# An encoder layer on one core: the order of everything outside the dense loop, chosen with another simulation

## The chip, the cores and the metric

One core of a Trainium2 chip runs the whole kernel. Its engines are TensorE (PE: matrix products), VectorE (DVE), ScalarE (ACT), GpSimd (POOL, here only for indirect loads) and SyncE (SP, here only for issuing DMAs). Each engine works through its own instruction queue in the order in which it was compiled, and waits at the head of that queue for the semaphores that the instruction needs. The metric is device time in microseconds (us) for one execution, as the median over runs.

## The reference

One layer of a streaming-encoder trunk for 1024 tokens of width 1024, in float32:

```
xn = rms_norm(h, norm1_g);  p = xn @ w_in          # split in xa, gate (512 each), us (512)
ya = rg_lru_group(xa, gate, ...)                   # conv, gates, first-order scan over time
yb = s5_group(us, ...)                             # state-space scan in chunks, GLU
h  = h + concat[rms_norm(ya), rms_norm(yb)] @ w_out
h  = h + peer_ffn(rms_norm(h))                     # below
out = rms_norm(h, normf_g)

# peer_ffn: 16384 single-neuron experts, 8 heads, 16 experts per token and head
q = x @ wq;  s1, s2 = q1 @ k1.T, q2 @ k2.T         # two sets of 128 scores per head
e, g = the 16 best of the sums s1 + s2, with softmax weights
act = gelu(u_tab[e] . x)
out = sum over (head, k) of g * act * v_tab[e]
```

## The kernel before, in words

The 1024 tokens are eight blocks of 128. Each block holds tokens of one half of the time axis, so that the second part can begin on the first half while the second half is still in work.

**Front** (`front`). The first norm, the input product, the S5 scan (`quarter`, four times), the LRU (`lru`, four times), the gates, the GLU, the two output norms and `w_out`. All large products are made in three passes from a high and a low part of each operand (`split_to`: ACT copies the high part, DVE subtracts to get the low one). `w_out` runs for the first four blocks, then the second half runs from `late`, `loads_late` and `norms_late`.

**PEER** (`peer`) works two ways. `NG` = 3 blocks are *gathered*: after the query and a top-k on DVE (`topk_gather`), POOL fetches one row of `peer_u` or `peer_v` per token and chosen expert by indirect DMA (tile `row`, eight buffers), and DVE multiplies and sums it (a `row` instruction for u; an accumulation into `hb` for v): 768 rows of 128 x 1024. `ND` = 5 blocks are *dense*: for these every expert is computed. `norm2` and `query` make `xDh`/`xDl` and the scores (`x2t`, `qp`, `S_d`), `build_g` makes the matrix of weights from one-hot tiles (`ohA`, `ohB`, `gp`, `gs`) and stores it in the DRAM tensor `G_d`, and `ahead` computes the activations of 97 of the 128 expert tiles beforehand (`ur` is loaded, split to `uh` and `ul`, multiplied into `ap`, evicted by ACT to `aa`, stored in the DRAM tensor `A_d`). The **dense loop** (`dense`) then runs over 32 groups of four tiles: it reads `A_d` back (`hr`), multiplies with the weights (`gt` from `G_d`, turned by ACT to `gq`), and multiplies by the rows of `peer_v` (`vp`, `total`). The rest of the gathered rows is spread through this loop.

What sets the order of the work:

- In the program text, the generators of the front and of PEER are merged by a planner (`Merge`), which has a cost for each kind of instruction, a clock for each engine and a bias for each generator; it always continues the one whose next step could start earliest. That gives the *trace order*.
- The tile framework then compiles the trace: outside blocks marked as manual, each engine's instructions are put in order by a list scheduler. It simulates the program, and whenever an engine is free it takes, of the instructions that the simulation holds ready, the one that stands first in the trace; one that is not ready is passed by. The same holds for the instructions that issue DMAs on the queues of SP, ACT and POOL. Buffers of the tile pools are handed out in that order too.
- The dense loop is written out by hand, and its order among its own instructions is kept:

```python
    mg.run([], until="g")
    weights(0)
    mg.run([], until="ahead")
    ...
    with tc.manual_schedule():
        dense()
```

All compute instructions pass one helper, so the profile gives them all line 146 and they are told apart by their tiles. Line 1170 is the indirect load, 1226 the load of `ur`, 1264 the store to `A_d`, 1131 the store to `G_d`, 1365 the reload `hr`, 1324 the load of `gt`, 1369 that of `vr`, 729 the load of the residual `h` on ACT's queue, 773 and 819 the loads of the weights of `w_out` and of the GLU, and 964 that of the query weights.

## Time and profile before

| | |
|---|---|
| Time, median of 3 runs | 2860.66 us (2846.72 to 2867.12) |
| The profiled execution | 2868.52 us, span 2866.7 us |
| Granted TensorE clock, mean | 0.944 |
| Busy: PE, DVE, ACT, POOL | 89%, 83%, 47%, 39% of the span |
| DMA | 767 MB, mean 268 GB/s |

The profile is of one execution. A row of a timeline has the start and the duration in us, then engine, line, operation, the written tile, the tiles read and how many were merged into the row; in square brackets stands the time for which the engine was idle before it and what ended that wait. A row of the waits has the waiting engine and tile, the one waited for, the total in us, how many times, and the longest. "q" behind an engine's name is its sequencer, which issues DMAs.

### The profile page before, as it was taken

The numbers are of one execution on the slowest core, as the hardware profiler recorded it, in microseconds if no ns is written. First come the engines' busy times: TensorE is split into PE (matmuls) and PEld (weight loads), VectorE is DVE, ScalarE is ACT, GpSimd is POOL, SyncE is SP. The second block draws the span as 40 slices with busy tenths as digits, with TensorE's granted clock in tenths as the row PEclk, the third lists the DMA queues.
The fourth block names the chain that finished last, engine by engine and source line by source line (L and its number), as shares of the span: only waits on it lengthen the run. The fifth ranks groups of instructions, "written<-read, shape, count | busy, mean of one in ns | idle before, by whom it ended". The sixth has DMA issues, their size and how long they took to land.

```text
span 2866.7 us, 40962 instructions
## 1 busy us (share of the span) xinstructions
PE 2549.5 (89%) x14623; PEld 2303.9 (80%) x14623; DVE 2383.2 (83%) x4582; ACT 1339.9 (47%) x2439; POOL 1131.2 (39%) x777
## 2 busy tenths in 40 slices
PE   6887787648889999899999968999899999999996
PEld 5765587448878899899989967888788888888884
DVE  7786543998889999999989847888788888988885
ACT  5355542122228568395774934443344443343332
POOL 0000000126825376673746533444344444444440
PEclk9989898869999999999999989999999999999998
DMA  5111444457969899899999988888789898988883
GB/s 163 25 28 33 124 144 130 153 181 238 383 240 338 286 362 386 320 371 362 361 363 316 346 314 274 312 314 315 274 311 316 314 313 312 328 316 310 312 310 106
DMA packets 305116, 767.21 MB, mean 268 GB/s; under 512 B 29328, under 2 KB 126928, under 8 KB 299792
## 3 DMA queue, kind: packets, MB, share of 16 engines
q0 software_dynamic: 110592, 402.70, 39.2%
q1 hardware_dynamic: 187168, 350.04, 35.2%
q10 hardware_dynamic: 7152, 11.85, 1.5%
q8 instruction: 115, 1.88, 0.2%
q14 instruction: 89, 0.73, 0.1%
HBM read 673.86 MB, written 89.46 MB: 266 GB/s over the span
## 4 chain that ended last, share of the span: by engine, by line
PE 58%; DVE 19%; DMA 11%; issue 6%; ACT 3%; POOL 2%; SPq 0%; ACTq 0%; DVEq 0%; POOLq 0%
PE vp L146 23%; PE ap L146 16%; PE total L146 6%; PE qp L146 3%; DMA A_d<-aa 3%; DVE row L146 3%; PE gp L146 3%; DVE ix L146 2%; POOL row L1170 2%; PE wop L146 1%; DMA ur<-in_uT_dram 1%; PE pj L146 1%; DVE ul L146 1%; DVE v L146 1%; DMA nf<-in_gf_dram 1%
## 5 line engine op out<-in xcount | busy, mean ns | idle before, releaser
L1170 POOL DMA_INDIRECT row<-in_peer_u_dram,idx x384 | 559.7, 1458 | 1037.6 <-DVE ix L146 505.8
L1170 POOL DMA_INDIRECT row<-in_peer_v_dram,idx x384 | 568.8, 1481 | 589.1 <-DVE hb L146 427.7
L146 PE MATMUL ap<-xDl,uh 128*128 128x320 f32 x2048 | 651.0, 318 | 54.7 <-ACT aa L146 32.8
L146 PE MATMUL ap<-xDh,ul 128*128 128x320 f32 x2048 | 643.3, 314 | 5.3 <-DVE ul L146 5.3
L146 PE MATMUL ap<-xDh,uh 128*128 128x320 f32 x2048 | 641.3, 313 | 0.3 <-issue 0.3
L146 DVE SCALAR_TENSOR_TENSOR hb<-row,act,hb 128x1024 f32<-128x1024 f32 x384 | 494.4, 1288 | 11.4 <-DMA row<-in_peer_v_dram,idx 4.6
L146 DVE CUSTOM_DVE_ANT_0 row<-row,xg 128x1024 f32<-128x1024 f32 x384 | 462.4, 1228 | 31.1 <-DMA row<-in_peer_u_dram,idx 20.5
L146 PEld LDWEIGHTS ap<-xDl,uh 128*128 128x128 f32 x2048 | 391.1, 191 | 58.7 <-ACT aa L146 35.3
L146 PE MATMUL vp<-vl,hh 128*128 128x512 f32 x1024 | 400.9, 391 | 15.2 <-DVE h L146 13.8
L146 PE MATMUL vp<-vh,hl 128*128 128x512 f32 x1024 | 400.5, 391 | 0.0
L146 PE MATMUL vp<-vh,hh 128*128 128x512 f32 x1024 | 400.2, 391 | 0.0
L146 PEld LDWEIGHTS ap<-xDh,ul 128*128 128x128 f32 x2048 | 390.6, 191 | 8.7 <-DVE ul L146 6.8
L146 PEld LDWEIGHTS ap<-xDh,uh 128*128 128x128 f32 x2048 | 389.8, 190 | 0.0
L146 ACT ACTIVATE gq<-gt 128x640 f32<-128x640 f32 x128 | 174.7, 1364 | 343.6 <-DVE hr L146 287.8
L146 DVE TENSOR_TENSOR ul<-ur,uh 128x1024 fp32r<-128x1024 f32 x128 | 157.3, 1229 | 104.7 <-ACT uh L146 104.6
L146 PEld LDWEIGHTS vp<-vl,hh 128*128 128x128 f32 x1024 | 193.3, 189 | 55.8 <-DVE h L146 14.7
L146 PEld LDWEIGHTS vp<-vh,hh 128*128 128x128 f32 x1024 | 193.4, 189 | 40.5
L146 PEld LDWEIGHTS vp<-vh,hl 128*128 128x128 f32 x1024 | 193.4, 189 | 39.4
L146 PE MATMUL gp<-ohB,ohA 128*128 128x128 f32 x1280 | 185.8, 281 | 29.5 <-DVE ohB L146 21.2
L146 ACT ACTIVATE ohB<-ohB,kt 128x128 f32<-128x128 f32 x480 | 206.8, 504 | 0.0
L146 ACT ACTIVATE aa<-ap 128x320 f32<-128x320 f32 x194 | 84.8, 440 | 246.7 <-PE ap L146 212.2
L146 PEld LDWEIGHTS gp<-ohB,ohA 128*128 128x128 f32 x1280 | 171.9, 195 | 34.0 <-issue 15.6
(415 smaller groups left out, 4626.9 us busy)
## 6 DMA issues: line engine op xcount, KB each, us to landing
ur<-in_uT_dram SPq DMA_DIRECT2D x128, 512.0 KB
vr<-in_peer_v_dram SPq DMA_DIRECT2D x128, 512.0 KB
G_d<-gs SPq DMA_DIRECT2D x20, 2048.0 KB
gt<-G_d SPq DMA_DIRECT2D x32, 1280.0 KB
A_d<-aa SPq DMA_DIRECT2D x97, 320.0 KB
hr<-A_d SPq DMA_DIRECT2D x96, 320.0 KB
wqr<-in_wq_dram SPq DMA_DIRECT2D x32, 512.0 KB
wor<-in_w_out_dram SPq DMA_DIRECT2D x32, 256.0 KB
```

Of the source, the lines that this page charges most:

```text
L146: return fn(*args, **kw)
L1170: G.indirect_dma_start(out=r, out_offset=None, in_=a["peer_v" if at >= P else "peer_u"], in_offset=bass.IndirectOffsetOnAxis(ap=idx[n][:, ...
```

## The change

The context that compiles the kernel is given one flag. With it the list scheduler drives another simulation: one that keeps a time line for each hardware resource (engines, queues, DMA engines) rather than the plain simulation of the cores. The program text, its trace order, all tiles and all buffer counts are the same; the dense loop is under manual schedule in both.

```diff
-    with _tile.TileContext(nc) as tc:
+    with _tile.TileContext(nc, schedule_with_timeline_sim=True) as tc:
         body(tc, args)
```

## The prediction

> **What bounds the kernel now.** I read the stretches of the span first, because the change leaves one part of the program alone and I need to know how long that part is. The columns are the stretch, then busy time and count on PE, its weight loads, DVE, ACT and POOL, the granted clock, the DMA share and GB/s.
>
> ```profile
> 0.00:290.00 290.00, 223.97 (x1360) 178.75 (x1360) 216.34 (x417) 141.43 (x229) 2.78 (x9) 0.91 0.23 64
> 290.00:475.00 185.00, 158.83 (x824) 143.83 (x824) 83.87 (x132) 85.48 (x145) 0.00 (x0) 0.92 0.43 128
> 475.00:610.00 135.00, 64.51 (x219) 48.29 (x220) 122.31 (x518) 26.90 (x40) 23.44 (x21) 0.71 0.49 167
> 610.00:790.00 180.00, 154.24 (x974) 148.19 (x973) 156.44 (x407) 42.16 (x90) 115.22 (x75) 0.91 0.79 281
> 790.00:1640.00 850.00, 795.78 (x5573) 787.23 (x5573) 803.39 (x2004) 565.32 (x1370) 488.78 (x312) 0.97 0.94 337
> 1640.00:1740.00 100.00, 63.98 (x403) 62.71 (x402) 52.92 (x54) 40.47 (x80) 33.61 (x25) 0.80 0.87 320
> 1740.00:2867.00 1127.00, 1088.21 (x5278) 934.89 (x5276) 947.89 (x1053) 438.14 (x487) 467.38 (x336) 0.98 0.84 296
> ```
>
> From about 1740 us the hand-written dense loop runs with PE busy 1088 of 1127 us; the order there is fixed, so it is worth nothing to this change. What the change can reach is 1740 us. In it PE is busy 224.0 + 158.8 + 64.5 + 154.2 + 795.8 + 64.0 = 1461 us, so 279 us are idle. The largest reachable stretch, 790 to 1640, has PE at 94%, DVE at 95% and the DMA engines at 94%: three resources full together, so another order has little to win there and something to lose. The loose places are 475 to 610 (PE 65 of 135) and the seam to the dense loop, 1640 to 1740 (PE 64 of 100).
>
> Next I looked for what an order can cause: an engine's queue whose head waits for a transfer while ready work stands behind it. At the seam, in the timelines of ACT, PE, SP and DVE:
>
> ```profile
> 1684.39 0.44 ACT L146 ACTIVATE aa<-ap 128x320 f32<-128x320 f32 x1 [2.13 <-PE ap L146]
> 1699.62 1.33 ACT L146 ACTIVATE gq<-gt 128x640 f32<-128x640 f32 x1 [14.80 <-DMA gt<-G_d]
> 1700.86 0.75 ACT L146 ACTIVATE aa<-ap 128x320 f32<-128x320 f32 x2
> 1701.33 0.64 PE L146 MATMUL ap<-xDl,uh 128*128 128x320 f32 x1 [9.94 <-ACT aa L146]
> 1701.31 7.17 SPq L1264 DMA_DIRECT2D A_d<-aa  x2
> 1710.45 0.80 SPq L1365 DMA_DIRECT2D hr<-A_d  x2
> 1713.72 0.83 DVE L146 TENSOR_TENSOR hr<-hr,gq 128x640 f32<-128x640 f32 x1 [30.21 <-DMA hr<-A_d]
> ```
>
> ACT stands 14.80 us before `gq<-gt`, the first copy of the dense loop, whose load has not landed. Two `aa` evictions of the pre-computed tiles stand behind it; PE waits 9.94 us for them. The last `A_d` stores therefore go out from 1701, the reload `hr<-A_d` at 1710, and DVE starts the dense loop after 30.21 us of waiting.
>
> The second place is the start of the dense blocks' norm:
>
> ```profile
> 573.67 0.75 DVE L146 SCALAR_TENSOR_TENSOR h<-wop,rg,h 128x512 f32<-128x512 f32 x1
> 575.62 1.06 ACT L146 ACTIVATE uh<-ur 128x1024 fp32r<-128x1024 f32 x1 [4.04 <-DMA ur<-in_uT_dram]
> 576.58 1.04 ACT L146 ACTIVATE jk<-h 128x1024 f32<-128x1024 f32 x1
> 581.25 0.17 DVE L146 TENSOR_SCALAR vv<-vv 128x5 f32<-128x5 f32 x1
> 583.79 1.06 ACT L146 ACTIVATE wqh<-wqr 128x1024 fp32r<-128x1024 f32 x1 [3.67 <-DMA wqr<-in_wq_dram]
> 584.88 1.23 DVE L146 TENSOR_TENSOR wql<-wqr,wqh 128x1024 fp32r<-128x1024 f32 x1 [3.34 <-ACT wqh L146]
> 586.03 0.16 DVE L146 TENSOR_TENSOR r<-r,vv 128x5 f32<-128x5 f32 x1
> 587.72 1.94 PE L146 MATMUL x2t<-ident,xn 128*128 128x128 f32 x8 [20.87 <-ACT wqh L146]
> 615.03 1.03 PE L146 MATMUL x2t<-ident,xn 128*128 128x128 f32 x8
> ```
>
> The last half of `h` is written at 574.4, but its square sum `jk` starts at 576.58, because a weight split `uh` that waited for its load is ahead of it: 2.2 us. The last factor of `r` is ready to compute at 581.4 and runs at 586.03, behind `wql`, which waits for a weight load: 4.6 us. PE has nothing for 20.87 us.
>
> **The change, part by part.** No arithmetic, tile, buffer count or DMA is added or removed. The dense block is written in manual order and keeps it. What moves is, on each engine and on the queues of SP, ACT and POOL, the place of instructions outside that block: the scheduler picks by trace order among what its simulation holds ready, and the change swaps the simulation that says when that is. The trace does not show the new order, so I bound its cost.
>
> Seam: if the finer simulation holds `gt` back for as long as the trace does, both `aa` go ahead of `gq`, and PE's last matmul group starts 9.94 us earlier; the `A_d` stores, the `hr` reload and the first dense product follow in a chain. `gq` is then late next: it still cannot start before 1699.6, and ends at 1700.9, which is earlier than `hr` would be (1713.7 − 9.9 = 1703.8), so the 9.9 us hold. Against a second seam delay stand the SP stores, shown by these rows of SP's timeline and one of the list of DMA issues:
>
> ```profile
> 1638.63 0.37 SPq L1131 DMA_DIRECT2D G_d<-gs  x1
> 1640.61 18.55 SPq L1264 DMA_DIRECT2D A_d<-aa  x1
> 1672.46 0.37 SPq L1131 DMA_DIRECT2D G_d<-gs  x1
> 1672.93 17.33 SPq L1264 DMA_DIRECT2D A_d<-aa  x1
> ...
> G_d<-gs SPq DMA_DIRECT2D x20, 2048.0 KB
> ```
>
> Each 2 MB `G_d` store makes the `A_d` issue behind it hold SP for 17 to 19 us, and the loads `ur`, `vr` and `gt` queue behind that. A new order can move these holds but not remove them; I cost them at nothing, covered as now by DVE's rows. [...]
>
> Norm: 2.2 + 4.6 = 6.8 us, if `jk` and `r` go ahead of the weight splits. DVE is 122 of 135 us busy here, but `r`, `xn` and `xDl` are short and come before everything PE can do next, so I take the 6.8 whole. If DVE puts rows or top-k steps in the freed place, nothing is left of it.
>
> Middle, 790 to 1640: here are PE's and ACT's waits of that stretch.
>
> ```profile
> PE gp L146 <- DVE ohB L146: 21.2, 4, 7.6
> PE ap L146 <- ACT aa L146: 19.0, 6, 7.9
> ACT aa L146 <- DMA A_d<-aa: 23.2, 4, 11.7
> ACT uh L146 <- DMA ur<-in_uT_dram: 10.2, 4, 8.0
> ```
>
> PE waits 19.0 us for `aa`, held in ACT's queue by a full store buffer. One of four such holds moved behind ready one-hot work would give about 5 us; I take 5. The ends are −19 (all of them) and +54, if the balance is lost and PE's idle time here (850 − 796 = 54) doubles; the value sits near zero because the engines are full.
>
> First 475 us: a hold of another kind stands there.
>
> ```profile
> 283.93 17.18 ACTq L729 DMA_DIRECT2D h<-in_x_dram  x16
> 301.15 0.63 ACT L146 ACTIVATE wgh<-wg 128x512 fp32r<-128x512 f32 x1 [16.17 <-DMA h<-in_x_dram]
> 303.88 0.77 PE L146 MATMUL wop<-wol,nh 128*128 128x512 f32 x1 [20.73 <-issue]
> ```
>
> Sixteen issues of `h` fill ACT's queue for 17.18 us while PE stands 20.73 us. They are earlier in trace order than `wgh` and ready together, so either simulation should pick them first: I cost this at 0. If the other simulation splits them up, it is worth up to 16 us.
>
> Sum: −9.9 − 6.8 − 5 = −21.7 us. The profiled execution took 2868.5 us for a span of 2866.7, and the sum makes it 2846.8. The median of the runs shown, 2860.66, lies 7.9 us under that execution; taken off the median it is **2839 us**, −0.76%. About 1% (28.6 us) is what the measurement can tell from no change.
>
> [...]
>
> **The rivals.**
> *No difference* (the order changes where it does not matter, or hardly at all). For it: the full middle, and trace order as the first key in both simulations. Against: at least three heads of queues wait for late transfers, so the present simulation is measurably too early. Time: 2861.
>
> *A much better front.* If all three long PE stalls quoted go, 9.94 + 20.87 + 20.73 = 51.5 us: 2809. Against: the 20.87 is mostly a chain through DVE, and the 20.73 is trace order.
>
> *Slower: other DVE work gets ahead of the norm chain.* The dense query and all 97 pre-computed tiles wait for `xDl`, and these five blocks share DVE with gathered rows and the top-k of the next blocks, which stand earlier in trace order.
>
> ```profile
> L1170 POOL DMA_INDIRECT row<-in_peer_u_dram,idx x384 | 559.7, 1458 | 1037.6 <-DVE ix L146 505.8
> L146 DVE CUSTOM_DVE_ANT_0 row<-row,xg 128x1024 f32<-128x1024 f32 x384 | 462.4, 1228 | 31.1 <-DMA row<-in_peer_u_dram,idx 20.5
> 543.78 4.46 DMA row<-in_peer_u_dram,idx
> 591.51 2.29 DVE L146 TENSOR_TENSOR oh<-pa__4521,i 128x2048 bf16<-128x2048 bf16 x1
> ```
>
> A row put ahead costs 1.23 us, a top-k step up to 2.29, and PE, at 94% afterwards, cannot win it back. From 23 rows (28.6 / 1.23) the loss passes 1%. POOL could issue (609 − 544) / 1.458 = 45 gathers before the query starts and issued 21 up to 610, so 24 more are possible: 30 us, plus some 7 us of top-k steps (three of 2.29), 37 in all: 2898. For it: a simulation that moves readiness moves all three kinds of work. Against: gathers that it sees as slower arrive later, which helps the norm.
>
> **How the numbers follow.** Forecast case 0.42, from −5 to −45 us, two fifths of it beyond 28.6. No difference 0.18; better front 0.16; slower 0.24, of which 0.01 stays under 28.6. Faster by over 1%: 0.17 + 0.16 = 0.33. Slower by over 1%: 0.23. Within 1%: 0.25 + 0.18 + 0.01 = 0.44. The range takes in the better front with the best middle (2861 − 51.5 − 19 = 2790) and, upwards, the slower case with a few us more, 2902; the far end of +54 in the middle, 2915, is left out. The forecast case's own range is 2816 to 2856.
>
> **What would show it.** Seam: `aa` directly before `gq` on ACT, no 9.94 us stall of PE, the wait for `hr<-A_d` under about 22 us. Norm: `jk` within 1 us of the last `h`, `r<-r,vv` not behind `wql`, PE's 20.87 us down to about 14. Middle: the same row counts and PE between 93% and 96%. Dense loop: 1127 us unchanged to within 3 us, since its order is fixed. The prediction is wrong if the start of the dense loop moves by more than 45 us either way, if rows pile up at the seam (many more `hb` steps between 1640 and 1740), if DVE runs a block of rows between `jk` and the first `xn`, or if the dense loop itself gets another length.

## The result: slower by 1.2%, and the profile after

The changed kernel took 2898.16 us (median of 4 runs, 2888.54 to 2902.95) beside 2861.23 us for the kernel before (4 runs): a ratio of 1.0122, 95% interval 1.0074 to 1.0171. The forecast was 2839 us; the time moved the other way. That it lies on the price of the slower rival, 2898, and so inside the range, is luck: the mechanism named there is not the one that acted, as the rows below show. The profiled execution took 2894.71 us for a span of 2892.9.

Two of the stretches of before, for the changed kernel (stretch, then busy time and count on PE, its weight loads, DVE, ACT and POOL, the granted clock, DMA share, GB/s):

```profile
790.00:1640.00 850.00, 825.87 (x5903) 822.37 (x5903) 758.01 (x1921) 591.85 (x1431) 375.96 (x264) 0.99 0.90 316
1640.00:1740.00 100.00, 0.00 (x0) 0.00 (x0) 85.22 (x102) 3.24 (x4) 78.02 (x64) 0.50 0.98 361
```

From 790 to 1640 PE is busy 825.87 us, where it was 795.78: the full middle became fuller. From 1640 to 1740 PE does nothing at all (x0), where it was busy 63.98 us, while DVE is busy 85.22 us. The seam, now in order of time, from the timelines of ACT, DVE and PE:

```profile
1622.46 0.44 ACT L146 ACTIVATE aa<-ap 128x320 f32<-128x320 f32 x1 [3.03 <-PE ap L146]
1623.02 1.23 DVE L146 CUSTOM_DVE_ANT_0 row<-row,xg 128x1024 f32<-128x1024 f32 x1 [1.24 <-DMA row<-in_peer_u_dram,idx]
1629.55 1.36 ACT L146 ACTIVATE gq<-gt 128x640 f32<-128x640 f32 x1 [6.65 <-DMA gt<-G_d]
1645.98 0.74 ACT L146 ACTIVATE hh<-hr 128x640 fp32r<-128x640 f32 x1 [15.08 <-DVE hr L146]
1648.84 1.22 DVE L146 CUSTOM_DVE_ANT_0 row<-row,xg 128x1024 f32<-128x1024 f32 x1
...
1738.51 5.35 DVE L146 SCALAR_TENSOR_TENSOR hb<-row,act,hb 128x1024 f32<-128x1024 f32 x4 [0.58 <-DMA row<-in_peer_v_dram,idx]
1743.77 0.82 DVE L146 TENSOR_TENSOR hr<-hr,gq 128x640 f32<-128x640 f32 x1
1744.62 0.74 ACT L146 ACTIVATE hh<-hr 128x640 fp32r<-128x640 f32 x1 [55.98 <-DVE hr L146]
1753.45 0.63 PE L146 MATMUL ap<-xDl,uh 128*128 128x320 f32 x1 [131.03 <-ACT uh L146]
```

and the two rows of before that answer to the first and the last of these:

```profile
1707.69 0.44 ACT L146 ACTIVATE aa<-ap 128x320 f32<-128x320 f32 x1 [6.08 <-PE ap L146]
1728.34 0.64 PE L146 MATMUL ap<-xDl,uh 128*128 128x320 f32 x1 [20.68 <-ACT uh L146]
```

The last `aa` is done at 1622.9, for 1708.1 before: in the new order the tiles that are computed ahead end 85.2 us earlier. But DVE is then still in gathered rows. The loop's order is fixed, and it contains rows of its own: ahead of the second `hr` in DVE's queue stands one, number 422, a step of `hb`. That sum is serial, so all rows traced before it must go first. DVE works them off from 1623 on (`row`, then `hb`), except for the first `hr`, until 1743, and only then multiplies the second `hr` (1743.77). ACT's `hh` waits 55.98 us for it, ACT's `uh` stands behind, and PE waits 131.03 us for `uh`. Before, the same wait was 20.68 us.

How fast the backlog goes is seen in two of the waits from 1623 to 1745 us:

```profile
POOL row L1170 <- issue: 21.6, 71, 0.3
DVE row L146 <- DMA row<-in_peer_u_dram,idx: 14.9, 16, 2.5
```

Between the last `aa` and the second `hr` DVE runs 77 rows in 121 us (the loop's own is the last), 1.57 us each. Its own work on them is 1.25 us each; the rest is mostly waiting for gathers (14.9 us for rows of u and 4.8 for rows of v). POOL in turn sends a gather every 1.57 us and waits for little but its own issuing. So a row left over costs more than its time on DVE: while the backlog is worked off, the gathers set the pace as well.

Where these rows come from is seen when the `row` and `hb` instructions of DVE are counted by stretch, first before, then after (stretch, DVE busy with rows and their count, then clock, DMA share and GB/s of the whole stretch):

```profile
1000.00:1200.00 200.00, 106.33 (x82) 0.99 0.97 355
1640.00:1760.00 120.00, 38.37 (x31) 0.83 0.83 297
```

```profile
1000.00:1200.00 200.00, 53.32 (x41) 1.00 0.81 268
1640.00:1760.00 120.00, 88.38 (x71) 0.50 0.98 365
```

Between 1000 and 1200 us, 41 rows instead of 82; between 1640 and 1760, 71 instead of 31. In the compiled order of DVE 421 rows stand before the last weight split of the 97 tiles in the old kernel and 336 in the new one; the other 85 stand between it and the loop's first split. In the middle POOL is not short of time: it waits for row buffers that DVE has not released (waits of 1000 to 1200, after and then before).

```profile
POOL row L1170 <- DVE hb L146: 50.8, 19, 4.6
```

```profile
POOL row L1170 <- DVE hb L146: 13.5, 9, 5.7
```

50.8 us now, 13.5 before. The loop itself is almost unchanged, which closes the account. First and last `total` of PE, before and after:

```profile
1751.45 0.39 PE L146 MATMUL total<-vl,hh 128*128 128x512 f32 x1
2842.99 0.39 PE L146 MATMUL total<-vh,hh 128*128 128x512 f32 x1
```

```profile
1776.86 0.39 PE L146 MATMUL total<-vl,hh 128*128 128x512 f32 x1
2870.42 0.39 PE L146 MATMUL total<-vh,hh 128*128 128x512 f32 x1
```

The loop starts 25.4 us later and is 2.0 us longer (1091.5 and 1093.6); what follows it is 1.2 us shorter. The sum, 26.2 us, is the difference of the spans (2892.9 − 2866.7). And of the 25.4, −85.2 us come from an earlier end of the tiles and +110.3 us from a longer stall (131.0 − 20.7); 0.3 us is left over.

### The profile page after: what moved, and what is told of

Read it like the earlier page. It is cut to its first block, busy times and chain, and to the rows that moved or that the text cites. A ratio compares the mean times of both kernels' runs of the same rounds, so it can differ in the third digit from the quotient of the medians.

```text
span 2892.9 us, 40980 instructions
## 1 busy us (share of the span) xinstructions
PE 2514.0 (87%) x14623; PEld 2276.8 (79%) x14623; DVE 2385.2 (82%) x4582; ACT 1348.0 (47%) x2442; POOL 1068.4 (37%) x777
## 4 chain that ended last, share of the span: by engine, by line
PE 59%; DVE 9%; issue 3%; DMA 3%; POOL 1%; SPq 0%; ACT 0%; DVEq 0%; POOLq 0%
PE ap L146 24%; PE vp L146 23%; PE total L146 6%; PE gp L146 4%; PE qp L146 2%; DVE hb L146 2%; DVE ul L146 1%; DMA nf<-in_gf_dram 1%; POOL row L1170 1%; DVE ix L146 1%; DVE oh L146 1%; DVE v L146 1%; DVE ohA L146 1%; DVE row L146 0%; PE sp L146 0%
## 5 line engine op out<-in xcount | busy, mean ns | idle before, releaser
L1170 POOL DMA_INDIRECT row<-in_peer_u_dram,idx x384 | 535.2, 1394 | 1041.1 <-DVE s L146 578.9
L1170 POOL DMA_INDIRECT row<-in_peer_v_dram,idx x384 | 530.4, 1381 | 684.5 <-DVE hb L146 455.5
L146 PE MATMUL ap<-xDl,uh 128*128 128x320 f32 x2048 | 648.5, 317 | 147.2 <-ACT uh L146 131.0
L146 PEld LDWEIGHTS vp<-vl,hh 128*128 128x128 f32 x1024 | 193.1, 189 | 59.3 <-DVE h L146 18.5
L146 PE MATMUL gp<-ohB,ohA 128*128 128x128 f32 x1280 | 199.5, 273 | 0.0
L146 PEld LDWEIGHTS gp<-ohB,ohA 128*128 128x128 f32 x1280 | 183.8, 190 | 0.0
L146 DVE TENSOR_TENSOR h<-h,vp 128x1024 f32<-128x1024 f32 x128 | 155.6, 1216 | 24.1 <-PE vp L146 24.1
```

The source lines that it names most:

```text
L146: return fn(*args, **kw)
L1170: G.indirect_dma_start(out=r, out_offset=None, in_=a["peer_v" if at >= P else "peer_u"], in_offset=bass.IndirectOffsetOnAxis(ap=idx[n][:, ...
```

## The experiments

**Theory A**: the loss is the backlog of rows at the seam; without it the new order is faster than the old. **Rivals**: the rows are only badly placed, and rows put first would cure it; or fewer rows help under any order, and the flag has no merit. All kernels compute the whole layer. "Rows" below are those traced before the dense loop; the others run inside it. The stall is PE's one wait `ap` for `uh` at the seam. Every ratio is to the kernel before, timed beside it.

**Fewer rows, with the flag and without it.** `PACE` is the interval at which the planner issues rows; 2.6 instead of 2.0 traces 354 rows ahead of the loop instead of 421.

```diff
-PACE = 2.0
+PACE = 2.6
-    with _tile.TileContext(nc) as tc:
+    with _tile.TileContext(nc, schedule_with_timeline_sim=True) as tc:   # only in the first of the two
```

> The changed scheduler, with the planner's pace constant 2.0 -> 2.6: 354 instead of 421 gathered rows are traced before the dense loop, the other 67 are spread through it. Theory A (backlog: the new order puts rows on DVE late, 85 of them stand between the 97th and 98th weight split, and the dense loop's first own row waits for them): the 131 us stall of PE at the seam falls by about 67 x 1.28 = 86 us to some 45, the dense loop carries 13.2 rows a group instead of 11.1 and gets 0 to 15 us longer; total 2815 to 2835. Theory B (the gathers themselves come in slower under the new order, whatever is traced where): the stall stays above 100 us, total 2880 to 2910.

> The scheduler of before, with the same pace constant 2.6 (354 rows traced before the dense loop). Control for e1. Theory A: there is no backlog here to remove, so the seam stays within 10 us of before; what moves is 86 us of DVE work out of a middle where DVE is 95% busy, against a denser loop: 2825 to 2865, that is, e1 gains at least twice as much over the changed kernel as this gains over before. Theory B: e1 and this move by the same amount.

With the flag: 2815.53 us, ratio 0.9802 (0.9779 to 0.9824). Without it: 2884.35 us, ratio 1.0043 (1.0019 to 1.0067). The waits at the seam of the first:

```profile
PE ap L146 <- ACT uh L146: 36.1, 1, 36.1
```

67 rows fewer took 95 us off the stall, 1.4 us each: between the 1.22 to 1.28 us that a row takes on DVE and the 1.57 us at which the backlog went. Without the flag the same edit gains nothing; it is even 0.4% slower, where 2825 to 2865 us was expected, although its stall is 20.3 us as expected. So the new order has a merit of its own, and the backlog hid it.

**A scale of doses.** The flag, with the gathers held at a fixed number of rows until the loop begins:

```diff
+CAP = 335          # and 380, 320
 def gate():
+    if not share and mg.units >= CAP:
+        return lambda: False
     return (lambda: mg.units < share[0]) if share else None
```

> The changed scheduler, with the gather thread of the planner held after 335 rows until the dense loop (433 left, 13.8 a group). Theory A: no backlog at all at the seam, PE's stall there 20 to 40 us, about as before; but DVE in the dense loop then needs 29.9 + 2.7 x 1.28 = 33.4 us of the 34.26 us period, so PE starts to wait there: 10 to 40 us longer than e1's loop or equal; total 2805 to 2840. Theory B: stall above 100 us, total 2880 to 2910.

> Dose for the backlog: the changed scheduler, the gather thread held after 380 rows (45 between the 97th and 98th weight split; 85 in the changed kernel, 22 in e1, 3 in e4). The stall of PE at the seam was 131.0 us with 421 rows, 36.1 with 354 and 20.4 with 335. Theory A (each row of the backlog costs its 1.28 us on DVE plus the gap to the next row, and all of it is PE's stall): 131 - 41 x 1.4 = about 74 us, total 2840 to 2858. If the stall is a step (some wait that is there or not), it is near 131 or near 36.

> The changed kernel with its gathered rows held at 320 until the dense loop, 15 fewer than in the run with 335 (2806.19 us, seam stall 20.4 us). Theory A (the loss is a backlog of rows at the seam, and 335 already removes it): the stall stays at about 20 us, the 15 rows are added to the loop at about their DVE time of 1.2 us, and where DVE has room there they cost nothing: 2803 to 2825 us. Rival (the number of rows before the loop itself sets the time, along a line through 421, 380, 354 and 335): another 10 us gained, about 2796, with the stall below 10.

| rows before the loop | stall, us | time, us | ratio (95%) |
|---|---|---|---|
| 421 (the change) | 131.0 | 2898.16 | 1.0122 (1.0074 to 1.0171) |
| 380 | 66.9 | 2840.45 | 0.989 (0.9856 to 0.9924) |
| 354 | 36.1 | 2815.53 | 0.9802 (0.9779 to 0.9824) |
| 335 | 20.4 | 2806.19 | 0.9767 (0.9744 to 0.979) |
| 320 | 20.4 | 2819.96 | 0.9831 (0.9783 to 0.9878) |

The seam waits with 380 and then with 335 rows:

```profile
PE ap L146 <- ACT uh L146: 66.9, 1, 66.9
```

```profile
PE ap L146 <- ACT uh L146: 20.4, 1, 20.4
DVE hr L146 <- DMA hr<-A_d: 17.3, 1, 17.3
```

The stall falls by 1.6 us per row from 421 to 380 and by 0.8 at the end, and stops at 20.4 us, where DVE waits for the transfer `hr` instead of for rows. Below that point a row held back only makes the loop longer: 15 more in it cost 13.8 us, 0.9 each, and the loop (first to last `total`) grew by as much, from 1110.1 to 1123.4. This is against the rival of the last run, a straight line through the counts. The times of all three runs are within what theory A gave. 335 is the best version of all: 2.3% under the kernel before, and by the two ratios (0.9767 / 1.0122) 3.5% under the changed one. It is also, within one, the count that the changed kernel had done by itself at the last weight split of the 97 tiles (336).

**Are the rows only badly placed?** The flag, with the two DVE instructions of a row at high priority:

```diff
+            with tc.high_priority():
                 V.tensor_tensor_reduce(ub, ub, xg, 1.0, 0.0, ALU.mult, ALU.add, act[:, k:k + 1])
...
+            with tc.high_priority():
                 V.scalar_tensor_tensor(hb, vb, act[:, k:k + 1], hb, ALU.mult, ALU.add)
```

> The changed scheduler, and the rows' two DVE instructions get high priority, so that a row that the simulation holds ready goes before everything else on DVE. If the rows are late because other DVE work stands before them in the order of the trace (theory C), the backlog goes and the total is 2865 or less. If they are late because the simulation does not hold them ready earlier, that is, it lets gathers land at a slow pace (theory A), the order hardly moves (349 instead of 336 rows before the 97th split): the stall falls by some 13 x 1.28 = 17 us, total 2875 to 2895.

2910.78 us, ratio 1.013 (1.0103 to 1.0158), with a stall of 114.7 us. Both expectations for the time were missed, though the stall fell by 16 us, near the 17 that theory A gave: the last `aa` came 29.8 us later than in the changed kernel (1652.7 for 1622.9). First in priority, the rows come just as slowly:

```profile
1000.00:1200.00 200.00, 49.63 (x39) 1.00 0.81 264
```

39 rows between 1000 and 1200 us, against 41. An instruction that has the first claim and is still not taken is one that the simulation does not hold ready. So the new simulation seems to pace the gather, the buffer and the row more slowly than the chip does. This is inferred from the order; what the simulation reckons for a gather was not read out.

**Is it the row inside the loop's head that holds PE?** The flag, without the three rows between the first tiles (they go to later groups):

```diff
         # dense(), ahead of the first group
-        row()
```

> The changed scheduler and all 421 rows before the loop, but the dense loop's three first own rows, which stand between its first tiles, are left to the groups (none is left out). Theory A, in its strict form (the loop starts late only because its first own row has to wait for the backlog): the four first tiles are then prepared at once, PE starts the loop within 40 us of its last tile, and waits for the backlog inside group 0, where the next own row stands after the first addition; the work of the backlog, some 85 x 1.28 us on DVE, still has to be done before that, so of the 131 us only 15 to 45 are saved: total 2850 to 2885. If it is the backlog's DVE work by trace order that holds even the first tiles back, nothing is saved: 2890 to 2905.

2881.58 us, ratio 1.0032 (1.0009 to 1.0054). The stall does not go, part of it moves to the first group of `vp`. The last row below counts DVE's `row` and `hb` instructions meanwhile:

```profile
1661.59 0.63 PE L146 MATMUL ap<-xDl,uh 128*128 128x320 f32 x1 [38.05 <-ACT uh L146]
1748.05 0.77 PE L146 MATMUL vp<-vl,hh 128*128 128x512 f32 x1 [66.90 <-issue]
```

```profile
1681.00:1748.00 67.00, 63.13 (x50) 0.52 1.02 402
```

38.05 + 66.90 = 105 us, of 131. The profile names no releaser for the second wait, but in its 67 us DVE runs 50 rows, and its weight split `vl` for that group only at 1746.68, 1.4 us before PE goes on. The time is within what the strict form of theory A gave. The backlog is not passed, it is worked off one step later.

**What shortened the middle?** From the end of the query to the last `aa`, the old kernel took 926 us and the changed one 857, for the same 5976 matmuls:

```profile
782.00:1708.00 926.00, 857.24 (x5976) 847.57 (x5975) 846.68 (x2051) 595.12 (x1439) 525.08 (x340) 0.96 0.94 338
```

```profile
766.00:1623.00 857.00, 835.82 (x5976) 832.12 (x5974) 765.05 (x1945) 594.87 (x1437) 378.96 (x265) 0.99 0.90 315
```

PE's idle time fell from 69 to 21 us, and its busy time by 21 too, at a granted clock of 0.99 for 0.96. Nearly all of the idle time that went was two kinds of waits of PE in that stretch, first before, then after:

```profile
PE ap L146 <- ACT aa L146: 32.8, 8, 9.9
PE gp L146 <- DVE ohB L146: 21.2, 4, 7.6
```

```profile
PE ap L146 <- ACT aa L146: 16.2, 5, 14.6
```

With two others of its kind, 4.1 us each, PE's waits for one-hot products (`gp`) come to 29.4 us before; in the changed kernel there is none, and the wait for evictions (`aa`) is half as long. The control without the flag (354 rows) took 920, so it is not the number of rows. Four causes were tried one by one on that control, each without the flag:

```diff
 # a: top-k of the dense blocks at high priority
+            with tc.high_priority(): ...        # every step of topk(b) in build_g
 # b: four store buffers
-            t = pk2.tile([P, TD], F32, name="aa", tag="aa", bufs=3)
+            t = pk2.tile([P, TD], F32, name="aa", tag="aa", bufs=4)
 # c: the 2 MB stores on ACT's queue, away from the A_d stores
-                nc.sync.dma_start(G_d[:, :, t0:t0 + GT]...
+                nc.scalar.dma_start(G_d[:, :, t0:t0 + GT]...
```

> The scheduler of before with 354 rows (as e2), and the top-k steps of the dense blocks traced at high priority, so that they come early on DVE, as they do under the changed scheduler (all eight top-k are done by the 10th weight split; by the 50th under the changed scheduler, the 80th before). The same 97 tiles and one-hot products took PE 926 us before, 920 in e2 and 857 under the changed scheduler. Theory M1 (what the changed scheduler won in the middle is that PE no longer waits for the next block's one-hot tiles, behind a top-k on DVE): 880 to 895 us, total 2830 to 2860. Theory M2 (it is the order of ACT's evictions and SP's stores): 915 to 925, total 2875 to 2890.

> The scheduler of before with 354 rows (as e2), and four buffers instead of three for the evicted tiles aa. In e2 PE waited 40.6 us for an eviction that itself waited for a buffer whose store to A_d stood behind a G_d store. Theory M2 (that wait is what the changed scheduler's order avoids): a fourth buffer covers another 9.5 us of each hold, PE's waits for aa fall to 10 to 20 us, the middle to 890 to 905, total 2850 to 2870. Theory M1: middle 910 to 925, total 2865 to 2890.

> The kernel before with the pace bias at 2.6 (as in the control with fewer rows, which took 2884.35 us and 920 us for the stretch of the 97 tiles, with 189 us of A_d issues on SP), and the 2 MB G_d stores issued on ACT's queue instead of SP's, so that no A_d store stands behind one. Theory S (the holds of SP behind G_d stores are what the new order shortened in that stretch): the A_d issues lose most of their 189 us, the stretch falls from 920 to about 870 us, and the time to about 2835. Rival (the holds are covered by the three store buffers and are not the cause): the holds go, the stretch stays within 15 us of 920, time 2870 to 2890. Third possibility: the hold moves to ACT, whose uh and aa then wait, and the time is above 2890.

a: 3015.6 us, ratio 1.0502 (1.0462 to 1.0543). DVE took the top-k first and starved PE of everything else, so this run says only that a burst of top-k is harmful:

```profile
790.00:1000.00 210.00, 68.42 (x385) 65.03 (x384) 201.88 (x1118) 34.08 (x59) 2.98 (x4) 0.66 0.19 71
```

b: 2875.76 us, ratio 1.002 (0.9999 to 1.0041), stretch again 920 us. ACT no longer waits for a store buffer, but now 43.2 us for the `ur` loads (2.2 in the control), and PE's wait for `aa` stays: 36.2 us for 40.6. c: 2915.01 us, ratio 1.0166 (1.0115 to 1.0218), stretch 960 us. What `c` did to SP shows in the issues of the `A_d` stores (shortest, median and longest, in ns), first of the control, then of c:

```profile
L1264 SPq DMA_DIRECT2D A_d<-aa x97: 319/320/24911, 802.3 to 1702.4; - x97
  ACT aa L146: 41.2, 2
```

```profile
L1264 SPq DMA_DIRECT2D A_d<-aa x97: 319/326/1225, 799.4 to 1739.1; - x97
  ACT aa L146: 8.9, 1
```

The longest hold fell from 24.9 to 1.2 us and ACT's waits for a store buffer from 41.2 to 8.9 us, and still the stretch became longer. PE's wait for `aa` did fall, from 40.6 to 6.3 us, but its waits for `gp` rose from 14.7 to 47.1, 18.5 of them behind `gs` copies on ACT; ACT itself waited 25.1 us for `G_d` stores. That is the third possibility of the expectation, a hold that moves to ACT. So neither b nor c took the hold away without putting another in its place, and whether the holds of SP bound the old order stays open. The same edit on the best version:

> The changed kernel with its gathered rows held at 335 until the dense loop (which took 2806.19 us, with the stretch of the 97 tiles at 856 us), and the G_d stores issued on ACT's queue. Theory S: there is little left to gain here, since the new order already spaced the stores; 2795 to 2806 us, stretch 845 to 856. If the hold moves to ACT: 2815 or more.

2810.78 us (2805.05 to 2814.38), ratio 0.9792 (0.9743 to 0.984): nothing to be measured. The longest hold fell from 13.1 to 0.6 us, and the stretch took 859 us with the edit and without it, so in the new order the holds are not what bounds it.

The fourth cause is the order of top-k and one-hot tiles. The `ohA` of each one-hot tile on DVE, counted by stretch, in the control and in the changed kernel:

```profile
1100.00:1200.00 100.00, 6.13 (x9) 0.98 0.94 339
1200.00:1300.00 100.00, 20.45 (x31) 1.00 0.91 307
1300.00:1400.00 100.00, 4.70 (x7) 0.91 0.94 356
```

```profile
1100.00:1200.00 100.00, 15.64 (x22) 1.00 0.83 269
1200.00:1300.00 100.00, 19.52 (x29) 1.00 1.00 362
1300.00:1400.00 100.00, 19.67 (x29) 1.00 0.98 349
```

In the control they come 9, 31 and 7 per 100 us: a block's one-hot tiles in a burst, then its successor's top-k, in which PE gets few one-hot products. In the changed kernel they come 22, 29 and 29. There top-k has run ahead: in DVE's compiled order the last step of the last top-k stands behind the 55th of the 97 weight splits, in the control behind the 72nd. The longest pause between two one-hot tiles is 11 us, in the control 86. To get such an order from the old simulation, each block's top-k and factors were traced ahead of the one-hot tiles of the block before:

```diff
-        for b in dblocks:
-            yield from build_g(b)
+        prev = None
+        for b in dblocks:
+            kt = yield from head_g(b)          # top-k, transposes, kt (two buffers)
+            if prev:
+                yield from tail_g(*prev)       # the one-hot tiles, gp, gs, G_d
+            prev = b, kt
+        yield from tail_g(*prev)
```

> The kernel before with the pace bias at 2.6, and the steps of the weight matrix regrouped: the top-k and transposed factors (kt, two buffers instead of one) of a dense block stand in the program ahead of the one-hot tiles of the block before. 362 rows are traced before the dense loop (354 in the control with fewer rows, 2884.35 us, whose stretch of the 97 tiles took 920 us). Theory P (in the new order top-k runs a block ahead, so that one-hot products are always there for PE, and that is what shortened the stretch): the stretch falls from 920 to 860 to 885 us and the time to 2815 to 2850. Rival (something else of the new order did it): the stretch stays within 15 us of 920 and the time at 2875 to 2895.

> As the kernel with top-k a block ahead under the old simulation, with the gathered rows held at 335 until the dense loop. Theory P: a seam stall of 20 us and 2805 to 2840 us, close to the changed kernel with 335 rows (2806.19), without the new simulation. Rival: 2870 to 2890.

> The changed kernel with 335 rows (2806.19 us, stretch 856 us), with top-k a block ahead in the program too. Theory P: the new simulation already runs top-k ahead, so nothing is left to gain: stretch 845 to 860, 2797 to 2812 us. Rival (what it did is something else and the two add up): the stretch falls below 840 and the time below 2795.

With 362 rows: 2844.02 us, ratio 0.9913 (0.9885 to 0.9942), 40 us under the control; with 335: 2856.48, ratio 0.9965 (0.9943 to 0.9986). Their stretches:

```profile
774.00:1675.00 901.00, 855.14 (x5972) 843.38 (x5970) 776.03 (x1967) 596.07 (x1438) 455.13 (x279) 0.98 0.87 311
```

```profile
783.00:1670.00 887.00, 847.66 (x5977) 839.31 (x5975) 745.22 (x1915) 596.28 (x1437) 398.04 (x253) 0.98 0.85 301
```

901 and 887 us, for 920 in the control and 857 in the changed kernel: the stretch came down by 19 and 33 us, where the theory asked for 35 to 60 and the rival for at most 15. So the regrouping gave 19 of the 63 us; the second kernel, with 33, also has 19 rows fewer in the stretch than the control, so its gain is not the regrouping's alone. And the mechanism is not shown: the edit did not make the even order, as pauses of up to 64 and 68 us between one-hot tiles remain. Nor is it clearly the wait for one-hot products that fell. PE's waits in the stretch, where the column of `gp` is a sum over all that it waited for:

| kernel | stretch, us | PE waits for `aa` | PE waits for `gp` |
|---|---|---|---|
| before | 926 | 32.8 | 29.4 |
| changed | 857 | 16.2 | 0 |
| control, 354 rows | 920 | 40.6 | 14.7 |
| b, four store buffers | 920 | 36.2 | 16.1 |
| c, stores on ACT's queue | 960 | 6.3 | 47.1 |
| regrouped, 362 rows | 901 | 11.8 | 20.0 |
| regrouped, 335 rows | 887 | 20.6 | 10.5 |

With 362 rows it was the wait for evictions that fell, and the wait for `gp` rose. What makes both small at once in the changed kernel stays open; that the one-hot tiles come without pauses there is the candidate. The first kernel's time fell as much as forecast, but only half of it in the stretch: 19 us there, 8 in the query before it, and 13 in a shorter loop (first to last `total` 1093.5, for 1106.9 in the control), which has 8 rows fewer in it. The second kernel missed its forecast of 2805 to 2840. The 335 rows do not help here: its loop (1714.27 to 2832.11) is 24 us longer than the first's (1717.99 to 2811.51) for 27 more rows in it, and its last `aa` only 5 us earlier. Under the flag the same edit adds nothing and rather harms: 2818.84 us, ratio 0.9831 (0.9787 to 0.9874), 12.7 us over the best version and above both forecasts, with a stretch of 871 us for 859 (the expectations have 856 for the best version; from its last `qp` to its last `aa` it is 859). Here pauses of 24 and 33 us between one-hot tiles came back.

## Why the prediction was wrong, point by point

**What failed.** The step that turned the sign is the seam: −9.9 us was forecast there, with the rows on DVE at no price, and the stall grew by 110.3 us, because 85 rows were left over. The middle was mis-sized the other way, with 69 us won where 5 were taken. With 16 us won up to the end of the query, 2.0 lost in the loop and 1.2 won after it, these make up the 26 us.

**The middle, "I take 5".** From the end of the query to the last `aa` 69 us were won, where 5, and the seam's 9.9 that lie in the same stretch, were forecast. The step was "three resources full together, so another order has little to win there". PE at 94%, DVE at 95% and DMA at 94% were read as three limits. But the 5976 matmuls can run in 857 us, and DVE's time contained rows that nothing in the stretch waits for. In the new order DVE is at 89% and PE at 98%. Fewer rows alone do not do it (the control: DVE 84%, PE still 93%), so it is the order; which part of it is shown only for a third of the gain, by the regrouping. A share of busy time over 850 us could not show that. The waits could: the row `PE gp <- DVE ohB: 21.2`, quoted just above the one that was priced, got no term, and it is gone in the changed kernel. The ends of this term, −19 to +54, came from PE's waits for one tile (`aa`, 19.0 us) and from doubling PE's idle time of 54 us; that the idle time itself could be won was not among them, and of the 69 us of it in the whole stretch 48 were.

**The backlog at the seam.** It was listed as what would make the prediction wrong ("if rows pile up at the seam"), with no price and no chance. It could have had both from the rows that were quoted: rows left over times 1.23 us on DVE. For the 85 of this order, which the old trace could not tell, that is 105 us; the stall grew by 110.3. That these are so near each other is partly chance: 9 of the 85 were done before the last `aa`, and the other 76 went at 1.57 us each. The text even held the cause ("gathers that it sees as slower arrive later") and counted it only as a help to the norm.

**The seam, −9.9.** The step itself happened: all `aa` precede `gq` (1622.46 and 1629.55), and the 9.94 us stall is gone. What was wrong is what is late next. It was given as `gq`; it was the second `hr`, behind DVE's rows. The holds "I cost them at nothing, covered as now by DVE's rows": the cover became the bound.

**The norm, −6.8.** It went the other way. The last `h` is ready 7 us earlier, at 567.2, and `jk` follows at 568.52, behind one `uh` of 1 us. But each short link of `r` then stands behind top-k steps and weight splits on DVE (four of its six links and what follows):

```profile
570.44 0.15 DVE L146 TENSOR_SCALAR vv<-ss 128x5 f32<-128x5 f32 x1
576.16 0.14 DVE L146 TENSOR_TENSOR vv<-vv,r 128x5 f32<-128x5 f32 x1
581.25 0.15 DVE L146 TENSOR_TENSOR vv<-vv,r 128x5 f32<-128x5 f32 x1
589.24 0.15 DVE L146 TENSOR_TENSOR r<-r,vv 128x5 f32<-128x5 f32 x1
590.58 2.46 DVE L146 SCALAR_TENSOR_TENSOR xn<-h,r,g 128x1024 f32<-128x1024 f32 x2
592.05 1.94 PE L146 MATMUL x2t<-ident,xn 128*128 128x128 f32 x8 [28.25 <-issue]
```

Six steps of about 0.15 us take 19 us, while DVE is busy without a gap (42.0 of the 42 us from 570 on), and PE starts the transposes at 592.05, 4.3 us later than before. This is the mechanism of the slower rival in small, with top-k steps and splits: the gathered rows that it priced at 30 us did not come. POOL's first gather of this stretch comes at 611 us, for 544 before:

```profile
611.20 2.89 POOL L1170 DMA_INDIRECT row<-in_peer_u_dram,idx  x1 [578.59 <-DVE s L146]
```

DVE ran 6 rows between 560 and 630 instead of 15, and the query, started later, ended 16 us earlier (last `qp` 766.1 for 782.1). The eight transposes took 1.94 us again after the long gap, at a granted clock of 0.50 from 570 to 612 us. In the kernel before, the same eight took 1.94 us at 0.50 too, and eight later ones (615.03) 1.03 us at 1.00.

**First 475 us, 0.** Right: the stall of 20.73 us is still there, at 19.7:

```profile
PE wop L146 <- issue: 19.7, 1, 19.7
```

**The dense loop, unchanged to 3 us.** Right, 2.0; but its length was taken as independent of what comes before it, and its first 100 us were not: the fixed order includes rows.

**The holds of SP.** That a new order "can move these holds but not remove them", and so costs nothing there, was the author's estimate. They were not gone in the changed kernel, but shorter: the longest `A_d` issue took 20.6 us before and 13.2 after. In the control it took 24.9 us, and 1.2 with the `G_d` stores on another queue. Nor did each store cost the 17 to 19 us of the rows quoted: in the same trace, of the `A_d` issues behind one, that at 1500.46 held SP for 4.44 us and that at 888.27 for 20.61.

## What to carry to other kernels

A full engine says little until its work is split into what the next stage needs and what is only filling: filler that is pushed out does not vanish, and an in-order block behind it pays for every piece, here 0.8 to 1.6 us per row. When a scheduler's order changes, ask of each stream of filler how much of it will be done by the time the fixed part begins, and price the remainder, by the slowest of the engines that it passes. A tuned count (421 rows) belongs to the order for which it was tuned: the same flag is 1.2% slower with 421 rows and 2.3% faster with 335.

## What was not expected of the hardware

An `A_d` issue behind a 2 MB `G_d` store on the same queue held SP for up to 24.9 us (control), and at most 1.2 us when that store went out on ACT's queue; of ACT's own 20 issues of it 18 took 0.37 to 0.39 us, the other two 2.6 and 6.5. And PE ran the same 5976 matmuls in 857 us at a granted clock of 0.99 and in 926 us at 0.96: with 48 us less of gaps, the work itself took 21 us less.
